# Adding the sums of the last down projection to the residual as each becomes whole, and moving the last norm's weights and factor one tile later

## The chip, the cores and the metric

The kernel runs on one core of a Trainium2 chip. The metric is device time in microseconds (us) of one execution. The engines are named as in the profile: PE is TensorE (matmuls; PEld its weight loads), DVE is VectorE, ACT is ScalarE, POOL is GpSimd, SP is SyncE, which here only issues DMAs. Each engine runs its instructions in order and waits on semaphores for the others. A change of 0.2% of the time, 1.7 us, is about the least that counts below as different.

## The reference

One encoder layer for two groups of 256 tokens (512 rows of 1024 numbers, float32), with shared weights, and a norm behind it:

```python
def rms_norm(x, g):
    y = x * lax.rsqrt(jnp.mean(x * x, axis=-1, keepdims=True) + EPS)
    return y * g

x = x + merged @ w_out                       # merged: three gated attention branches
h2 = rms_norm(x, norm2_g)
x = x + jnp.square(jax.nn.relu(h2 @ w_up)) @ w_down
return rms_norm(x, final_norm_g)
```

All that the change touches lies in the last three lines: the MLP, from 1024 to 4096 hidden units and back, the residual add, and the final norm.

## The kernel before

The attention part ends near 515 us of the span. The MLP behind it goes through the 4096 hidden units in NC = 8 chunks `c` of 512. Each matmul operand is split into two parts, a high and a low one (`hi`, `lo`; tiles `w` for weights, `f` and `h` for activations), and a product takes three matmuls (`mm3`), so the low part of a weight block, made by DVE, must be there for the second matmul of the first group.

Per chunk, eight half steps h = 0 to 7 compute the hidden units (`up`, matmuls `ps<-h,w`). Between them the down projection of the chunk before is done (`product`, matmuls `ps<-w,f`, 12 for each of seven products): Strassen's scheme in Winograd's form, with the token rows in two halves and the output columns in two halves, so that the output is four blocks "11", "12", "21", "22" (row half, column half), each of two row tiles of 128. The seven products go to four pairs of PSUM banks; a second product adds onto a bank pair that DVE has read before. `add_to` adds a bank to one of the sums in SBUF: "11", "12", "21" (tiles `acc`), "V" and "G", where V belongs to three outputs: 12 + V, 21 - V and 22 = G + V. The additions are put in the list `later` and are issued behind the next matmuls (`flush`).

The down projection of the last chunk, c = 7, is done without that scheme (`last_down`): for column half `hh` = 0 and then 1, and row tiles t = 0 to 3, twelve matmuls of 512 columns each; the last of them, hh = 1 and t = 3, is cut into two parts of 256 columns.

The residual rows lie in DRAM (`x1d`) until `fetch_x1` loads them into four `blk` tiles, `xt[t]` with the two column halves, and the final norm's weights into `gf`. The rows lack the factor of the norm ahead of the MLP, which is applied to the sums instead: `scaled` is one DVE instruction, a SCALAR_TENSOR_TENSOR, y = src * rr[t] + y. `combine` first adds V to (or takes it from) a sum, a TENSOR_TENSOR `acc<-acc,acc`, and then calls `scaled` on the result:

```python
    SUMMED = {5: "22", 6: "12", 7: "11"}
...
            if n != "11":
                V.tensor_tensor(acc[k, i], acc[k, i], acc["V", i], op=ALU.subtract if n == "21" else ALU.add)
            scaled(xt[t][:, int(n[1]) - 1], t, acc[k, i])
```

So in chunk 7 the sums 22, 12 and 11 are combined at half steps 5, 6 and 7, and 21 behind the first `last_down`.

The end is `finish` for each tile and half, and `final` for each tile. `finish`: DVE adds the bank (`blk<-ps,rr,blk`), ACT squares it with a running sum (`junk<-blk`, into `fs`), and DVE multiplies by the norm's weights (`blk<-blk,gf`), which must wait until ACT has read the tile. `final`: DVE sums `fs` (TENSOR_REDUCE) and scales it (TENSOR_SCALAR), POOL raises it to -1/2 (`fr`), ACT multiplies column half 0 by it and DVE half 1 (`blk<-blk,fr`), and ACT and SP each issue the store of one half.

Order: DVE, ACT and PE keep the order in which the program is written; SP's DMAs stand where their buffers are expected to come free.

Of the kernel before, what the change touches and what calls it, by code (L numbers as in the profile page):

```python
# [16 lines left out]
P = 128  # L17
# [60 lines left out]
def encoder_kernel(ctx: ExitStack, tc: tile.TileContext, a: dict, out: bass.AP):  # L78
# [68 lines left out]
    def unit(fn, *srcs):  # L147
        units.append((fn, srcs))
# [687 lines left out]
    ss = const("ss", [P, NT, 2])  # L836
    rr = const("rr", [P, NT])
    fs = const("fs", [P, NT, 3])
# [20 lines left out]
    def inv_ms():  # L859
        V.tensor_tensor(rr, ss[:, :, 0], ss[:, :, 1], op=ALU.add)  # L860
        V.tensor_scalar(rr, rr, 1.0 / D, EPS, op0=ALU.mult, op1=ALU.add)
        V.reciprocal(rr, rr)

# [104 lines left out]
    def product(w, c, name):  # L968
        _, bk, to, sign = PRODUCTS[name]
        x = forms.pop((c, name))  # L970
        new = name in ("P1", "Q5", "Q6", "P7")
        for i in range(2):
            if new:
                banks[bk, i] = bank()
            p = banks[bk, i]
            for j in range(2):
                t = slice(j * S + i * P, j * S + (i + 1) * P)
                k = slice(j * 512, (j + 1) * 512)
                mm3(p, x[:, 0, t], x[:, 1, t], w[0][:, k], w[1][:, k], new and j == 0, j == 1, not new)
        flush(9)  # L980
        ps_ = [banks[bk, i] for i in range(2)]
        later.append(lambda: [add_to(to, i, ps_[i], ALU.add if sign > 0 else ALU.subtract) for i in range(2)])

# [10 lines left out]

    def scaled(y, t, src):
        V.scalar_tensor_tensor(y, src, rr[:, t:t + 1], y, op0=ALU.mult, op1=ALU.add)


    def combine(n):
        k = "G" if n == "22" else n  # L1000
        for i in range(2):
            t = 2 * (n[0] == "2") + i
            if n != "11":
                V.tensor_tensor(acc[k, i], acc[k, i], acc["V", i], op=ALU.subtract if n == "21" else ALU.add)
            scaled(xt[t][:, int(n[1]) - 1], t, acc[k, i])

# [7 lines left out]
    def last_down(hh, ts, n0=0, n1=512, part=0):  # L1014
# [35 lines left out]
    for c in range(NC):  # L1050
        for h in range(8):
            ff, half = 4 * c + h // 2, h % 2
            unit(lambda *w, ff=ff, half=half: up(w[0] if w else None, ff, half), *([(a["w_up"][ff],)] if half == 0 else []))
            if c == 0:
                unit(lambda h=h: turn_x1(h % 4, h // 4))
            if h == 1:
                unit(lambda c=c: load_blocks(c) if c < NC - 1 else fetch_x1())
            if c == NC - 1 and h == 6:
                unit(lambda: ahead.__setitem__(0, 2))
            if c == NC - 1 and h in SUMMED:  # L1060
                unit(lambda n=SUMMED[h]: later.append(lambda: combine(n)))
            if c and h < 7:
# [11 lines left out]
    unit(lambda: later.append(lambda: combine("21")))  # L1074
    for t in (2, 3):
# [83 lines left out]
```

## Time and profile before

| | |
|---|---|
| time, median of 3 runs | 865.38 us (865.13 to 866.48) |
| the profiled execution's own time | 866.86 us |
| its span, first to last instruction | 865.1 us |
| PE busy | 845.0 us, 98% |
| DVE busy | 464.4 us, 54% |
| ACT busy | 397.8 us, 46% |
| POOL busy | 215.8 us, 25% |
| granted TensorE clock, mean | 0.989 of full |

The span is what instructions cover; the execution's own time is 1.8 us more. Busy shares are means over all stages. What a stage is worth is read from the stage itself: which engine waits there, and for whom. Times in the trace count from the start of the span.

### The profile page before, as it was taken

The numbers are of one execution on the slowest core, as the hardware profiler recorded it, in microseconds if no ns is written. First come the engines' busy times: TensorE is split into PE (matmuls) and PEld (weight loads), VectorE is DVE, ScalarE is ACT, GpSimd is POOL, SyncE is SP. The second block draws the span as 40 slices with busy tenths as digits, with TensorE's granted clock in tenths as the row PEclk, the third lists the DMA queues.
The fourth block names the chain that finished last, engine by engine and source line by source line (L and its number), as shares of the span: only waits on it lengthen the run. The fifth ranks groups of instructions, "written<-read, shape, count | busy, mean of one in ns | idle before, by whom it ended". The sixth has DMA issues, their size and how long they took to land.

```text
span 865.1 us, 10788 instructions
## 1 busy us (share of the span) xinstructions
PE 845.0 (98%) x4080; PEld 703.2 (81%) x4080; DVE 464.4 (54%) x741; ACT 397.8 (46%) x690; POOL 215.8 (25%) x161
## 2 busy tenths in 40 slices
PE   9999999999999999999999999999999999999993
PEld 8788998888888888888887888888888888888882
DVE  6585535465453312333436551556767676666884
ACT  6455555566554433223224346564544445454523
POOL 2314545656557452211222000000000010100001
PEclk9999999999999999999999999999999999999997
DMA  8343223224331238422322446475647465745212
GB/s 283 114 123 100 67 93 95 89 74 115 96 107 54 69 111 277 124 80 92 122 87 74 154 129 204 103 200 122 183 110 195 105 188 126 181 131 145 74 50 97
DMA packets 47468, 106.87 MB, mean 124 GB/s; under 512 B 19358, under 2 KB 19604, under 8 KB 47416
## 3 DMA queue, kind: packets, MB, share of 16 engines
q1 hardware_dynamic: 39992, 85.69, 30.5%
q0 software_dynamic: 4256, 14.73, 9.6%
q10 hardware_dynamic: 3168, 5.77, 1.9%
q8 instruction: 32, 0.52, 0.3%
q14 instruction: 20, 0.16, 0.1%
HBM read 101.93 MB, written 4.24 MB: 123 GB/s over the span
## 4 chain that ended last, share of the span: by engine, by line
PE 76%; DVE 12%; ACT 6%; issue 3%; DMA 2%; POOL 0%; SPq 0%; POOLq 0%; DVEq 0%; ACTq 0%
PE ps L72 69%; DVE w L72 3%; PE sc L72 3%; PE o L72 2%; ACT w L72 2%; PE tp L72 2%; DVE blk L72 2%; DVE acc L72 2%; DMA mr<-in_memT 1%; DVE f L72 1%; DMA raw<-in_w_mem 1%; ACT sp L72 1%; ACT junk L72 1%; DVE sp L72 1%; ACT f L72 1%
## 5 line engine op out<-in xcount | busy, mean ns | idle before, releaser
L72 PE MATMUL ps<-x,w 128*128 128x512 f32 x1080 | 252.4, 391 | 0.0
L72 PEld LDWEIGHTS ps<-x,w 128*128 128x128 f32 x1080 | 200.8, 188 | 41.4
L72 PE MATMUL ps<-h,w 128*128 128x512 f32 x768 | 184.5, 390 | 0.0
L72 PEld LDWEIGHTS ps<-h,w 128*128 128x128 f32 x768 | 143.6, 188 | 29.6
L72 PE MATMUL ps<-w,f 128*128 128x512 f32 (+1 forms) x696 | 164.4, 387 | 1.4 <-DVE acc L72 1.0
L72 DVE TENSOR_TENSOR w<-raw,w 128x1024 fp32r<-128x1024 f32 (+1 forms) x79 | 96.3, 1223 | 115.2 <-ACT w L72 114.8
L72 PEld LDWEIGHTS ps<-w,f 128*128 128x128 f32 x696 | 128.5, 188 | 30.5 <-issue 3.4
L72 ACT ACTIVATE w<-raw 128x1024 fp32r<-128x1024 f32 (+2 forms) x116 | 119.7, 1037 | 21.8 <-DMA raw<-in_w_mem 7.4
L161 POOL TENSOR_TENSOR w<-raw,w 128x1024 fp32r<-128x1024 f32 (+1 forms) x37 | 87.4, 2362 | 120.2 <-ACT w L72 95.0
L72 DVE TENSOR_TENSOR w<-blk,w 128x1024 fp32r<-128x1024 f32 x49 | 59.4, 1223 | 48.7 <-ACT w L72 48.7
L921 POOL DMA_DIRECT2D blk<-in_w_dn x21 | 18.2, 866 | 240.7 <-DVE w L72 240.7
L72 DVE TENSOR_TENSOR acc<-acc,ps 128x512 f32<-128x512 f32 x88 | 56.7, 681 | 2.7 <-PE ps L72 2.7
L72 ACT ACTIVATE w<-blk 128x1024 fp32r<-128x1024 f32 x49 | 50.8, 1049 | 15.9 <-DMA blk<-in_w_dn 15.9
L72 ACT ACTIVATE sp<-sp,st 128x256 f32<-128x256 f32 (+1 forms) x48 | 25.8, 539 | 57.7 <-DVE st L72 57.7
L72 ACT ACTIVATE f<-f 128x512 fp32r<-128x512 f32 x28 | 17.7, 633 | 74.3 <-DVE f L72 74.3
L72 ACT ACTIVATE g<-ps 128x512 f32<-128x512 f32 x16 | 9.6, 598 | 86.9 <-PE ps L72 86.9
L72 DVE TENSOR_TENSOR sum<-o,lo 64x256 f32<-64x256 f32 x24 | 10.0, 418 | 66.4 <-ACT lo L72 66.3
L72 PE MATMUL ps<-mg,w 128*128 128x512 f32 x192 | 44.3, 390 | 1.5 <-ACT mg L72 0.9
L72 PEld LDWEIGHTS ps<-mg,w 128*128 128x128 f32 x192 | 36.0, 188 | 9.6 <-ACT mg L72 1.3
L72 ACT ACTIVATE r<-ps 128x512 f32<-128x512 f32 x32 | 18.9, 591 | 52.4 <-PE ps L72 52.4
L72 PE MATMUL ps<-w,x 128*128 128x384 f32 (+1 forms) x192 | 39.9, 363 | 0.0
L469 POOL TENSOR_TENSOR sp<-sp,st 128x512 f32<-128x512 f32 (+1 forms) x32 | 36.7, 1148 | 6.4 <-DVE st L72 3.5
(147 smaller groups left out, 957.0 us busy)
## 6 DMA issues: line engine op xcount, KB each, us to landing
raw<-in_w_up SPq DMA_DIRECT2D x32, 512.0 KB, 4.5
blk<-in_w_dn SPq DMA_DIRECT2D x28, 512.0 KB, 7.3
blk<-in_w_dn POOLq DMA_DIRECT2D x28, 512.0 KB, 5.7
raw<-in_w_g SPq DMA_DIRECT2D x24, 512.0 KB, 3.3
raw<-in_w_b SPq DMA_DIRECT2D x12, 512.0 KB, 3.3
raw<-in_w_bam SPq DMA_DIRECT2D x8, 512.0 KB, 3.2
raw<-in_w_o SPq DMA_DIRECT2D x8, 512.0 KB, 3.2
raw<-in_w_mem SPq DMA_DIRECT2D x7, 512.0 KB, 3.8
```

The lines of the kernel that those rows point to most:

```text
L72: return self.tc.keep_in_program_order(method(*args, **kw))
L161: sub[0].tensor_tensor(lo[:, c], raw[:, c], f(hi[:, c]), op=ALU.subtract)
L469: G.tensor_tensor(s[:, :, :w], s[:, :, :w], st[:, 6:8].unsqueeze(2).to_broadcast([P, 2, w]), op=ALU.mult)
L921: G.dma_start(src, block(c, n[1:]), accum_op=ALU.add)
```

## The change

Three things change in the MLP's end.

1. In chunk 7 the sums go into the residual one by one. The sums of chunks 0 to 5 for 12, 11 and 21 are added to `xt` at half steps 1, 2 and 3; V at steps 4 (to 12) and 5 (from 21, with a factor -rr, for which `rr` gets a second column); G at step 6; V to 22 behind the first `last_down`. The last chunk's own products for 11, 12 and 21 are added from their banks to `xt` directly, by `scaled`, and no longer to `acc`. No `acc<-acc,acc` is left.
2. `fetch_x1` is called at the end of chunk 6 rather than in step 1 of chunk 7.
3. `finish` no longer multiplies by `gf`. Half 0 is multiplied by `gained`, one tile later; half 1 in `scale_out`, by one SCALAR_TENSOR_TENSOR with both the factor and `gf`. `final` is split into `factor` and `scale_out`, and `scale_out` of a tile stands behind the `finish` of the next one.

```diff
+        r, n = rr[:, :, 0], rr[:, :, 1]
...
+        V.tensor_scalar(n, r, -1.0, None, op0=ALU.mult)
...
+        if c == NC - 2 and to in ("11", "12", "21"):
+            later.append(lambda: sum_in(to, lambda i: ps_[i]))
+        else:
+            later.append(lambda: [add_to(to, i, ps_[i], ALU.add if sign > 0 else ALU.subtract) for i in range(2)])
...
+    def scaled(y, t, src, less=0):
+        V.scalar_tensor_tensor(y, src, rr[:, t, less:less + 1], y, op0=ALU.mult, op1=ALU.add)
+
+    def sum_in(n, src, less=0):
+
         for i in range(2):
             t = 2 * (n[0] == "2") + i
-            if n != "11":
-                V.tensor_tensor(acc[k, i], acc[k, i], acc["V", i], op=ALU.subtract if n == "21" else ALU.add)
-            scaled(xt[t][:, int(n[1]) - 1], t, acc[k, i])
+            scaled(xt[t][:, int(n[1]) - 1], t, src(i), less)
+
+    def combine(n, k, less=0):
+        sum_in(n, lambda i: acc[k, i], less)
...
-            if hh and n1 == 512:
-                later.append(lambda t=t: final(t, 2 + part))
+        t = ts[-1]
+        if hh and not part:
+            later.append(lambda: scale_out(t - 1) if t else None)
+        if hh and n1 == 512:
+            later.append(lambda: factor(t, 2 + part))
+        if hh == 0 or t == 0:
+            later.append(lambda: gained(t + hh * NT - 1))
...
-        V.tensor_tensor(y, y, gf[0][:, hh, n0:n1], op=ALU.mult)
...
+    def gained(t):
+        y = xt[t][:, 0]
+        V.tensor_tensor(y, y, gf[0][:, 0], op=ALU.mult)
...
+    def scale_out(t):
+        r = fr[:, t:t + 1]
         A.activation(xt[t][:, 0], xt[t][:, 0], AF.Copy, scale=r)
-        V.tensor_scalar(xt[t][:, 1], xt[t][:, 1], r, None, op0=ALU.mult)
+        V.scalar_tensor_tensor(xt[t][:, 1], xt[t][:, 1], r, gf[0][:, 1], op0=ALU.mult, op1=ALU.mult)
...
-    SUMMED = {5: "22", 6: "12", 7: "11"}
+
+    SUMMED = {1: ("12", "12"), 2: ("11", "11"), 3: ("21", "21"), 4: ("12", "V"), 5: ("21", "V", 1), 6: ("22", "G")}
...
-            if h == 1:
-                unit(lambda c=c: load_blocks(c) if c < NC - 1 else fetch_x1())
+            if h == 1 and c < NC - 1:
+                unit(lambda c=c: load_blocks(c))
+            if h == 7 and c == NC - 2:
+                unit(fetch_x1)
```

Where the instructions stand, on DVE in steps 3 to 5 of chunk 7. First the kernel before; `acc_4663` and `acc_4665` are V, `acc_4760` and `acc_4762` are G, `ps_6703` and `ps_6710` the bank pair that the last product, matmuls `ps_6703<-w_6717,f_6700`, goes on to use, `w_6718` that product's low weights.

```order
L72 TENSOR_TENSOR w_6696<-raw_6694,w_6695 128x1024
L72 TENSOR_TENSOR f_6700<-u_6427,f_6700 128x512
L72 TENSOR_TENSOR w_6718<-blk_6240,w_6717 128x1024
L72 TENSOR_TENSOR acc_4760<-acc_4760,ps_6703 128x512
L72 TENSOR_TENSOR acc_4762<-acc_4762,ps_6710 128x512
L72 TENSOR_TENSOR acc_4760<-acc_4760,acc_4663 128x512
L72 SCALAR_TENSOR_TENSOR blk_6557<-acc_4760,rr,blk_6557 128x512
L72 TENSOR_TENSOR acc_4762<-acc_4762,acc_4665 128x512
L72 SCALAR_TENSOR_TENSOR blk_6559<-acc_4762,rr,blk_6559 128x512
L72 TENSOR_TENSOR w_6759<-raw_6757,w_6758 128x1024
```

The same place with the change; `acc_4664` and `acc_4666` are V now, `acc_4761` and `acc_4763` are G, and `blk_6488` to `blk_6494` the rows of tiles 0 to 3.

```order
L72 TENSOR_TENSOR w_6703<-raw_6701,w_6702 128x1024
L72 TENSOR_TENSOR f_6707<-u_6428,f_6707 128x512
L72 SCALAR_TENSOR_TENSOR blk_6488<-acc_4664,rr,blk_6488 128x512
L72 SCALAR_TENSOR_TENSOR blk_6490<-acc_4666,rr,blk_6490 128x512
L72 TENSOR_TENSOR w_6727<-blk_6241,w_6726 128x1024
L72 TENSOR_TENSOR acc_4761<-acc_4761,ps_6710 128x512
L72 TENSOR_TENSOR acc_4763<-acc_4763,ps_6717 128x512
L72 SCALAR_TENSOR_TENSOR blk_6492<-acc_4664,rr,blk_6492 128x512
L72 SCALAR_TENSOR_TENSOR blk_6494<-acc_4666,rr,blk_6494 128x512
L72 TENSOR_TENSOR w_6766<-raw_6764,w_6765 128x1024
```

Two additions of V now stand ahead of the last product's weights and of the reading of its bank pair; behind that pair four instructions became two.

DVE's last rows, from the last whole tile (t = 2, half 1) on. Before; `blk_6557` is tile 2, `blk_6559` tile 3, the `ps` their banks.

```order
L72 SCALAR_TENSOR_TENSOR blk_6557<-ps_6955,rr,blk_6557 128x512
L72 TENSOR_TENSOR blk_6557<-blk_6557,gf_6561 128x512
L72 TENSOR_REDUCE fr<-fs 128x1
L72 TENSOR_SCALAR fr<-fr 128x1
L72 TENSOR_SCALAR blk_6557<-blk_6557,fr 128x512
L72 SCALAR_TENSOR_TENSOR blk_6559<-ps_6979,rr,blk_6559 128x256
L72 TENSOR_TENSOR blk_6559<-blk_6559,gf_6561 128x256
L72 SCALAR_TENSOR_TENSOR blk_6559<-ps_6996,rr,blk_6559 128x256
L72 TENSOR_TENSOR blk_6559<-blk_6559,gf_6561 128x256
L72 TENSOR_REDUCE fr<-fs 128x1
L72 TENSOR_SCALAR fr<-fr 128x1
L72 TENSOR_SCALAR blk_6559<-blk_6559,fr 128x512
```

With the change; `blk_6490` is tile 1, `blk_6492` tile 2, `blk_6494` tile 3.

```order
L72 SCALAR_TENSOR_TENSOR blk_6492<-ps_6950,rr,blk_6492 128x512
L72 SCALAR_TENSOR_TENSOR blk_6490<-blk_6490,fr,gf_6496 128x512
L72 TENSOR_REDUCE fr<-fs 128x1
L72 TENSOR_SCALAR fr<-fr 128x1
L72 SCALAR_TENSOR_TENSOR blk_6494<-ps_6973,rr,blk_6494 128x256
L72 SCALAR_TENSOR_TENSOR blk_6492<-blk_6492,fr,gf_6496 128x512
L72 SCALAR_TENSOR_TENSOR blk_6494<-ps_6993,rr,blk_6494 128x256
L72 TENSOR_REDUCE fr<-fs 128x1
L72 TENSOR_SCALAR fr<-fr 128x1
L72 SCALAR_TENSOR_TENSOR blk_6494<-blk_6494,fr,gf_6496 128x512
```

The multiplications by `gf` behind ACT's square are gone, and a tile's scaling stands behind the next bank's addition.

SP's queue in chunk 7, the one place where it differs; first before, then with the change. `raw` are weights on their way in, `gf` the norm's weights.

```order
L165 DMA raw_6506<-in_w_up 128x1024
L990 DMA blk_6559<-x1d 128x1024
L165 DMA raw_6607<-in_w_up 128x1024
L165 DMA raw_6694<-in_w_up 128x1024
L992 DMA gf_6561<-in_gf 128x1024
```

```order
L165 DMA raw_6517<-in_w_up 128x1024
L995 DMA blk_6494<-x1d 128x1024
L997 DMA gf_6496<-in_gf 128x1024
L165 DMA raw_6610<-in_w_up 128x1024
L165 DMA raw_6701<-in_w_up 128x1024
```

The loads of the residual rows stay where they were; `gf` moved ahead of two loads of weights.

## Rows read from the trace of the kernel before

**Rows 1.** The page: the span and its instructions.

```profile
span 865.1 us, 10788 instructions
```

**Rows 2.** Busy time by stretch: length, PE, PEld, DVE, ACT, POOL, clock, DMA.

```profile
850.20:865.10 14.90, 0.00 (x0) 0.00 (x0) 5.92 (x17) 4.63 (x11) 1.66 (x3) 0.58 0.37 141
```

**Rows 3.** PE's timeline from chunk 7's last product: start, length, instruction, count.

```profile
822.23 2.88 PE L72 MATMUL ps<-w,f 128*128 128x512 f32 x12
...
827.67 22.50 PE L72 MATMUL ps<-w,f 128*128 128x512 f32 x108
...
846.91 3.26 PE L72 MATMUL ps<-w,f 128*128 128x512 f32 x25
```

**Rows 4.** DVE's timeline, 797 to 836 us; in brackets the idle time before, and its releaser.

```profile
798.50 0.69 DVE L72 TENSOR_TENSOR f<-u,f 128x512 fp32r<-128x512 f32 x1 [1.13 <-ACT f L72]
800.90 1.23 DVE L72 TENSOR_TENSOR w<-blk,w 128x1024 fp32r<-128x1024 f32 x1 [1.71 <-ACT w L72]
...
806.72 1.23 DVE L72 TENSOR_TENSOR w<-blk,w 128x1024 fp32r<-128x1024 f32 x1 [0.26 <-ACT w L72]
...
813.21 1.23 DVE L72 TENSOR_TENSOR w<-blk,w 128x1024 fp32r<-128x1024 f32 x1 [0.26 <-ACT w L72]
...
818.42 1.28 DVE L72 TENSOR_TENSOR acc<-acc,ps 128x512 f32<-128x512 f32 x2
819.61 0.69 DVE L72 TENSOR_TENSOR acc<-acc,acc 128x512 f32<-128x512 f32 x1
...
822.39 1.22 DVE L72 TENSOR_TENSOR w<-raw,w 128x1024 fp32r<-128x1024 f32 x1
...
825.32 1.22 DVE L72 TENSOR_TENSOR w<-raw,w 128x1024 fp32r<-128x1024 f32 x1
...
831.76 0.68 DVE L72 TENSOR_TENSOR f<-u,f 128x512 fp32r<-128x512 f32 x1
...
834.63 0.74 DVE L72 SCALAR_TENSOR_TENSOR blk<-ps,rr,blk 128x512 f32<-128x512 f32 x1
```

**Rows 5.** Timeline of all engines, 853 us to the end.

```profile
853.13 0.74 DVE L72 SCALAR_TENSOR_TENSOR blk<-ps,rr,blk 128x512 f32<-128x512 f32 x1
...
854.66 0.69 DVE L72 TENSOR_TENSOR blk<-blk,gf 128x512 f32<-128x512 f32 x1 [0.79 <-ACT junk L72]
...
858.29 0.48 DVE L72 SCALAR_TENSOR_TENSOR blk<-ps,rr,blk 128x256 f32<-128x256 f32 x1
858.80 0.42 ACT L72 ACTIVATE junk<-blk 128x256 f32<-128x256 f32 x1 [0.89 <-DVE blk L72]
...
859.34 0.42 DVE L72 TENSOR_TENSOR blk<-blk,gf 128x256 f32<-128x256 f32 x1 [0.57 <-ACT junk L72]
859.69 0.15 DVE L72 TENSOR_REDUCE fr<-fs 128x1 f32<-128x3 f32 x1
...
860.69 0.72 ACT L72 ACTIVATE blk<-blk,fr 128x512 f32<-128x512 f32 x1 [1.37 <-POOL fr L1036]
...
861.44 0.34 ACTq L72 DMA_DIRECT2D out<-blk  x1
```

**Rows 6.** DVE's groups by shape, 790 to 865 us: count, busy us, mean ns, idle before.

```profile
L72 DVE TENSOR_TENSOR acc<-acc,ps 128x512 f32<-128x512 f32 x14 | 8.9, 680 | 0.0
...
L72 DVE SCALAR_TENSOR_TENSOR blk<-acc,rr,blk 128x512 f32<-128x512 f32 x8 | 5.9, 750 | 0.2
...
L72 DVE TENSOR_TENSOR blk<-blk,gf 128x512 f32<-128x512 f32 x7 | 4.9, 694 | 5.5 <-ACT junk L72 5.5
...
L72 DVE TENSOR_SCALAR blk<-blk,fr 128x512 f32<-128x512 f32 x4 | 1.9, 486 | 2.7 <-POOL fr L1036 2.7
```

**Rows 7.** SP's queue, 777 to 794 us: issues of x1d, weights and gf.

```profile
777.39 0.32 SPq L990 DMA_DIRECT2D blk<-x1d  x1
779.72 10.75 SPq L165 DMA_DIRECT2D raw<-in_w_up  x2
790.52 0.42 SPq L992 DMA_DIRECT2D gf<-in_gf  x1
```

More of the change, by code (lines that the diff above doesn't have):

```diff
@@ L836, in encoder_kernel @@
     ss = const("ss", [P, NT, 2])
-    rr = const("rr", [P, NT])
+    rr = const("rr", [P, NT, 2])
     fs = const("fs", [P, NT, 3])
@@ L859, in inv_ms @@
     def inv_ms():
-        V.tensor_tensor(rr, ss[:, :, 0], ss[:, :, 1], op=ALU.add)
-        V.tensor_scalar(rr, rr, 1.0 / D, EPS, op0=ALU.mult, op1=ALU.add)
-        V.reciprocal(rr, rr)
+        r, n = rr[:, :, 0], rr[:, :, 1]
+        V.tensor_tensor(r, ss[:, :, 0], ss[:, :, 1], op=ALU.add)
+        V.tensor_scalar(r, r, 1.0 / D, EPS, op0=ALU.mult, op1=ALU.add)
+        V.reciprocal(r, r)
+        V.tensor_scalar(n, r, -1.0, None, op0=ALU.mult)
     UP, blocks = {}, {}
@@ L981, in product @@
         ps_ = [banks[bk, i] for i in range(2)]
-        later.append(lambda: [add_to(to, i, ps_[i], ALU.add if sign > 0 else ALU.subtract) for i in range(2)])
+        if c == NC - 2 and to in ("11", "12", "21"):
+            later.append(lambda: sum_in(to, lambda i: ps_[i]))
+        else:
+            later.append(lambda: [add_to(to, i, ps_[i], ALU.add if sign > 0 else ALU.subtract) for i in range(2)])
     xt, gf, kept = {}, [], {}
@@ L993, in fetch_x1 @@
         gf.append(g)
[L995 to L1000, printed above, removed]
+    def scaled(y, t, src, less=0):
+        V.scalar_tensor_tensor(y, src, rr[:, t, less:less + 1], y, op0=ALU.mult, op1=ALU.add)
+    def sum_in(n, src, less=0):
         for i in range(2):
             t = 2 * (n[0] == "2") + i
-            if n != "11":
-                V.tensor_tensor(acc[k, i], acc[k, i], acc["V", i], op=ALU.subtract if n == "21" else ALU.add)
-            scaled(xt[t][:, int(n[1]) - 1], t, acc[k, i])
+            scaled(xt[t][:, int(n[1]) - 1], t, src(i), less)
+    def combine(n, k, less=0):
+        sum_in(n, lambda i: acc[k, i], less)
     def down(p, t, hh, ks, n0=0, n1=512):
@@ L1029, in finish, with factor @@
         A.activation(h2("junk")[:, n0:n1], y, AF.Square, accum_out=fs[:, t, at_:at_ + 1])
-        V.tensor_tensor(y, y, gf[0][:, hh, n0:n1], op=ALU.mult)
-    def final(t, n):
+    def gained(t):
+        y = xt[t][:, 0]
+        V.tensor_tensor(y, y, gf[0][:, 0], op=ALU.mult)
+    def factor(t, n):
         r = fr[:, t:t + 1]
@@ L1060, in encoder_kernel @@
             if c == NC - 1 and h in SUMMED:
-                unit(lambda n=SUMMED[h]: later.append(lambda: combine(n)))
+                unit(lambda n=SUMMED[h]: later.append(lambda: combine(*n)))
             if c and h < 7:
@@ L1073, in encoder_kernel @@
          *[(block(NC - 1, n),) for n in ("11", "21")])
-    unit(lambda: later.append(lambda: combine("21")))
+    unit(lambda: later.append(lambda: combine("22", "V")))
     for t in (2, 3):
@@ L1082, in encoder_kernel @@
         unit(lambda n=part: last_down(1, (3,), 256 * n, 256 * n + 256, n))
-    unit(lambda: flush(9))
+    unit(lambda: (flush(9), scale_out(NT - 1)))
     run()
```

## The prediction

> **What bounds the kernel now.** First the span [rows 1], then the busy time by stretch, then the timelines of PE and DVE side by side. PE is busy for 98% of the span, so in most of it nothing but PE matters. The exception is the end: from 850.20 to 865.10 us PE does nothing, and DVE (5.92 us), ACT and POOL share the stretch at low busy shares [rows 2]. PE's last matmul ends at 846.91 + 3.26 = 850.17 [rows 3]. DVE begins to read that matmul's bank only at 858.29 [rows 5]. So the last 15 us are two things: 8.1 us in which DVE, which works in order, is still busy with earlier banks, and 6.8 us from there to the end of the span, a chain that any version must go through (add the bank, square, sum, power, scale, store, end of program).
>
> Why DVE is late: it reads the first bank of the last projection at 834.63 [rows 4], and from there each tile and half costs it an addition, a wait for ACT's square (5.5 us over seven additions of 512 columns) and a multiplication by the norm's weights, and each tile a wait for POOL's power besides (2.7 us in four) [rows 6]. That is more than the 2.72 us that PE needs for twelve matmuls (822.23 to 827.67 is two such rows [rows 3]): DVE falls behind, and the last whole tile's bank, full at 846.91 + 0.39 = 847.3, is read at 853.13 [rows 3, 5].
>
> PE itself loses a little here too: from 827.67 to 846.91 there are 83 starts (the row of 108 less the row of 25) [rows 3]. At 2.72/12 = 0.227 us they make 18.81, not 19.24: 0.43 us are lost. The place is the low part of the last hidden units, which DVE makes at 831.76 to 832.44 [rows 4]; PE wants it for the third of its matmuls on k = 3, the 21st, at 827.67 + 20 x 0.227 = 832.21, and 0.3 of the loss is this.
>
> **What the change does to DVE in chunk 7.** Count the instructions of 512 columns for the sums: before, 6 additions from a bank to `acc`, 6 of V, 8 `scaled`; after, 6 `scaled` from a bank and 14 from `acc`. 20 and 20. So no work vanishes; 6 TENSOR_TENSORs of 0.69 and 6 of 0.68 become SCALAR_TENSOR_TENSORs of 0.75 [rows 4, 6], and eight of the twenty move ahead, to half steps 1 to 4. Two of 0.68 take 1.19 start to start (818.42 to 819.61 [rows 4]): the next starts 0.08 before the end. So I count a pair of 0.75 as 1.34.
>
> I follow DVE's lag against the trace of before [rows 4]. The pair of step 1 goes into the idle 1.13 ahead of 798.50; the 0.2 left over ends in the 1.71 ahead of 800.90. The first product onto a bank is added by `scaled`: +0.13. The pair of step 2 has 0.26 + 0.1 idle time ahead of 806.72: lag 1.1. The pair of step 3: ACT's hidden units behind it are as late as DVE, and of the pair only some 0.05 more remains: lag 1.15 at 813.21. The pair of step 4 has no idle time: lag 2.5. Then it goes back: at 819.61 four instructions (2.78) become two (1.34): lag 1.05 at 822.39, 1.2 at 825.32 with the next bank pair. Between 826.46 and 831.76, eight instructions (5.30) become four (2.68): DVE is 1.4 us ahead at 831.76, at 830.34.
>
> Is PE held by this lag? Low weights of the last product but one: wanted at 822.23 - 5.44 + 0.23 = 817.0, done 813.21 + 1.15 + 1.23 = 815.6. Bank pair of the last product, which DVE must have read: wanted at 822.23 [rows 3], first half read at 818.42 + 2.5 + 0.68 = 821.6, **0.6 us to spare**, the tightest place. Weights of the last projection, second block: wanted at 827.67 + 7 x 0.227 = 829.26, done 825.32 + 1.2 + 1.22 = 827.74. All in time, so the cost is nothing, covered by PE's stream; without that cover each us of lag is a us. And the low part at 831.76 comes 1.4 us earlier, so PE's 0.43 loss goes. PE would end at 849.74.
>
> **What it does to DVE at the end.** The two weight splits behind follow at 830.94; the second waits for its load, which is issued when the buffer is free, 1.2 us later than before, and ends near 833.2. The first bank is added at 833.2 instead of 834.63. Then two additions (1.34), the multiplication of tile 0, which waits for ACT's square (1.53 behind the addition, as 853.13 to 854.66 [rows 5]), two additions of V, the third tile, the multiplication of tile 1: 838.0. Tile 3's bank is full at 827.67 + 48 x 0.227 + 0.16 = 838.7. **From here DVE waits for PE**, and has per tile of 2.72 us: addition 0.67, scaling of the tile before 0.67, sum and scale 0.36, and one `gained` in front of it at most.
>
> Is the fused scaling, two tensors and a factor, 0.75? No row has it with `gf`. Bounds: 0.49, the one-tensor scaling that it replaces, and 0.75, the `scaled` of the same size [rows 6]. I take 0.75, since it reads two tensors too. On the path it counts little: the store of half 0 waits for ACT's 0.72 [rows 5], and half 1's is issued by SP, 0.26 later than before, at the same time as ACT's; between 0 and 0.3 us, and I take 0. The Trainium skill, VectorE: DVE Perf Modes, "The perf-mode tier table", speaks against this fusion: float32 instructions on one SBUF tensor have a mode of twice the rate, those on two tensors have not. The trace agrees, 0.49 beside 0.69 [rows 6]; by the rule the sum below is at most 0.3 us too low, by the rows' 0.72 of ACT it stands.
>
> The last tiles: tile 2's bank is full when PE starts on the 256-column parts, at 846.91 + 0.39 - 0.43 = 846.87; added at 846.9; sum at + 1.53 = 848.45; factor ready 1.00 behind that, as 859.69 to 860.69 [rows 5]: 849.45. The first part's addition starts at 848.8; the scaling of tile 2 waits for its factor, 849.45 to 850.13; the last part's addition, whose bank was full at 849.79, starts at 850.13, **0.34 us late instead of 8.1**. ACT has the scaling of tile 2 (0.72) and its store's issue (0.34) ahead of the last square, so that starts at 850.98, not 850.64. The sum follows the square by 0.54 (858.80 to 859.34), without the multiplication that stood between (0.35); factor at 850.98 + 0.54 + 1.00 = 852.52.
>
> **The sum**, against ACT's last scaling at 860.69 [rows 5]: DVE's lateness, 8.08 to 0.34: -7.74; PE's loss: -0.43; the multiplication ahead of the last sum: -0.35; ACT's scaling and store ahead of the last square: +0.34. Together -8.2: 852.5, and with the 4.4 us from there to the end a span of 856.9. The profiled execution took 866.86 with a span of 865.1, and the median of the runs shown is 865.38; I take 8.2 off that: **857.2 us**.
>
> What I cost at nothing besides: the extra factor -rr (one small DVE instruction in chunk 0, some 0.15 us by its kin, under PE's stream); `fetch_x1`, whose loads stand where they stood, the last at 777.39, while the first addition into a row is at 797.3 [rows 4, 7]; POOL's four powers, same count; POOL's last block load, which is issued behind the split at 800.90, ahead of any lag.
>
> **The rivals.**
> *The early additions hold PE.* Against 0.6 us to spare, the eight additions of steps 1 to 4 would have to be 0.1 us longer each to cost 0.2, or the pair of step 1 find its idle time gone (another 1.3, cost 0.7). For it: four SCALAR_TENSOR_TENSORs now stand where idle time was only 0.26. Time 857.4 to 859.0; what PE loses, the end loses whole.
> *A new wait at the end.* ACT's queue holds square, scaling and store issue of two tiles; if the store issue or a power is later than in the rows, tile 2's scaling holds DVE ahead of the last addition. Each 0.3 us is 0.3 us: up to 858.5.
> *The change does not do it.* If DVE's waits were not what makes the end late but some fixed cost behind PE, the span would not move: 865. Against it: POOL's and ACT's waits are named in the rows, and the last bank waits 8.1 us for DVE alone.
> *Slower: `gf` blocks SP's queue.* Its load now stands ahead of two loads of weights, and it waits for a buffer that PE must have read. If the buffer came free late, the weights behind it would be late: they were issued at 779.72, and are needed by PE after 808. The load and the two splits take some 7 us, so it costs PE from a release after about 801, us for us; slower than before from a release after 809. Against it: in the trace `gf` goes out at 790.52 right behind the weights, with a buffer one step later in the rotation, and the built program's wait is for the 3448th of 3952 matmuls, 504 from the last, some 110 us before PE's end.
>
> **How the numbers follow.** My forecast, 856.5 to 857.9 us, has 0.72; PE held by the additions or a new wait, to 859.0, has 0.20 together; no effect 0.03; `gf` 0.03, slower; the remaining 0.02 lies below 856.5 or between 859 and 863. The range 856.3 to 859.0 holds the first two. Within 0.2% (1.7 us) is about what a measurement here cannot tell from no change; only the case of no effect falls there. Faster 0.94, same 0.03, slower 0.03.
>
> **What would show it.** Right: PE without a gap at 832 and done near 849.8; DVE idle, released by PE, ahead of each `blk<-ps,rr,blk` from 838 on; the last of them within 0.5 us of PE's end; no DVE wait for ACT's square but ahead of sums. Wrong: a PE wait for DVE's `acc` near 822; `blk<-ps` still following each other without a wait for PE; SP's weight loads later than 779.7 and 790.1.

## The result, and the profile after

The changed kernel takes 858.0 us (median of 4 executions, 857.19 to 859.08) against 865.9 for the kernel before on the same chip: a ratio of 0.991, 95% interval [0.989, 0.993]. Run once more, 857.58 against 865.22, again 0.991 [0.9895, 0.9925]. Predicted were 857.2, 856.3 to 859.0. The profiled execution took 859.08, with a span 7.8 us shorter than before [rows 1]. The page's first line, and the waits from 795 to 858 us (total, times, longest):

```profile
span 857.3 us, 10785 instructions
```

```profile
DVE blk L72 <- PE ps L72: 3.1, 4, 1.4
...
DVE fr L72 <- ACT junk L72: 1.7, 2, 0.9
...
DVE blk L72 <- POOL fr L1049: 0.9, 2, 0.7
...
PE ps L72 <- DVE acc L72: 0.2, 1, 0.2
```

Read the first of the waits: in the last projection DVE now waits for PE, four times. No DVE `blk` waits for ACT's square any more; before, seven additions had cost 5.5 us in such waits, and POOL's power 2.7 [rows 6]. PE's only wait in this stretch, 0.2, is at 794.91, ahead of the first addition that moved (797.27); the kernel before has the same wait, 0.17 at 794.93. Of the six banks from 838 on DVE waits for PE ahead of four (3.1 us in all); the two parts of 256 columns were whole before DVE came to them. The tail in which PE does nothing is about 7.6 us instead of 14.9 [rows 2]; by stretch (length, PE, PEld, DVE, ACT, POOL, clock, DMA):

```profile
849.60:857.30 7.70, 0.10 (x1) 0.00 (x0) 2.03 (x5) 2.18 (x6) 0.55 (x1) 0.67 0.48 183
```

PE's timeline, which answers to [rows 3]. The 108 matmuls are one row of 22.07, not 22.50, and the gap at 832 is gone:

```profile
822.19 2.88 PE L72 MATMUL ps<-w,f 128*128 128x512 f32 x12
...
827.63 22.07 PE L72 MATMUL ps<-w,f 128*128 128x512 f32 x108
```

DVE's timeline, for [rows 4]. Compare the starts of the same instructions: 806.72 is now 807.88, 813.21 is 814.36, the bank pair of 818.42 is at 820.89, 822.39 is 823.41, 825.32 is 826.47, the low part of 831.76 is at 830.25, and the first bank, read at 834.63 before, is read at 833.24:

```profile
807.88 1.22 DVE L72 TENSOR_TENSOR w<-blk,w 128x1024 fp32r<-128x1024 f32 x1
...
814.36 1.22 DVE L72 TENSOR_TENSOR w<-blk,w 128x1024 fp32r<-128x1024 f32 x1
...
820.89 1.28 DVE L72 TENSOR_TENSOR acc<-acc,ps 128x512 f32<-128x512 f32 x2
...
823.41 1.22 DVE L72 TENSOR_TENSOR w<-raw,w 128x1024 fp32r<-128x1024 f32 x1
...
826.47 1.22 DVE L72 TENSOR_TENSOR w<-raw,w 128x1024 fp32r<-128x1024 f32 x1
...
830.25 0.69 DVE L72 TENSOR_TENSOR f<-u,f 128x512 fp32r<-128x512 f32 x1
...
833.24 1.40 DVE L72 SCALAR_TENSOR_TENSOR blk<-ps,rr,blk 128x512 f32<-128x512 f32 x2
...
838.71 0.75 DVE L72 SCALAR_TENSOR_TENSOR blk<-ps,rr,blk 128x512 f32<-128x512 f32 x1 [0.66 <-PE ps L72]
```

The last tiles in the timeline of all engines, for [rows 5]. The last bank is added at 850.09, 0.39 behind PE's end (827.63 + 22.07 = 849.70); the time in brackets at 849.42 is the wait for tile 2's power that holds it:

```profile
846.88 0.75 DVE L72 SCALAR_TENSOR_TENSOR blk<-ps,rr,blk 128x512 f32<-128x512 f32 x1 [0.84 <-PE ps L72]
...
849.42 0.75 DVE L72 SCALAR_TENSOR_TENSOR blk<-blk,fr,gf 128x512 f32<-128x512 f32 x1 [0.27 <-POOL fr L1049]
...
850.09 0.48 DVE L72 SCALAR_TENSOR_TENSOR blk<-ps,rr,blk 128x256 f32<-128x256 f32 x1
850.57 0.34 ACTq L72 DMA_DIRECT2D out<-blk  x1
850.96 0.42 ACT L72 ACTIVATE junk<-blk 128x256 f32<-128x256 f32 x1 [0.41 <-DVE blk L72]
...
851.50 0.15 DVE L72 TENSOR_REDUCE fr<-fs 128x1 f32<-128x3 f32 x1 [0.93 <-ACT junk L72]
...
852.51 0.72 ACT L72 ACTIVATE blk<-blk,fr 128x512 f32<-128x512 f32 x1 [1.04 <-POOL fr L1049]
852.51 0.75 DVE L72 SCALAR_TENSOR_TENSOR blk<-blk,fr,gf 128x512 f32<-128x512 f32 x1 [0.66 <-POOL fr L1049]
853.26 0.37 ACTq L72 DMA_DIRECT2D out<-blk  x1
```

DVE's groups by shape, 790 to 857 us, for [rows 6]:

```profile
L72 DVE SCALAR_TENSOR_TENSOR blk<-ps,rr,blk 128x512 f32<-128x512 f32 x13 | 9.4, 748 | 3.1 <-PE ps L72 3.1
...
L72 DVE SCALAR_TENSOR_TENSOR blk<-blk,fr,gf 128x512 f32<-128x512 f32 x4 | 3.0, 749 | 0.9 <-POOL fr L1049 0.9
```

SP's queue, for [rows 7]. The load of `gf` is issued ahead of the two loads of weights, without a wait in front of it:

```profile
777.11 0.32 SPq L995 DMA_DIRECT2D blk<-x1d  x1
777.48 0.42 SPq L997 DMA_DIRECT2D gf<-in_gf  x1
779.44 11.00 SPq L165 DMA_DIRECT2D raw<-in_w_up  x2
```

### The profile page after: what moved, and what is told of

It reads as the page before. It is cut to its first block, busy times and chain, and to the rows that moved or that the text cites. A ratio compares the mean times of both kernels' runs of the same rounds, so it can differ in the third digit from the quotient of the medians.

```text
span 857.3 us, 10785 instructions
## 1 busy us (share of the span) xinstructions
PE 844.4 (99%) x4080; PEld 703.8 (82%) x4080; DVE 462.8 (54%) x737; ACT 397.1 (46%) x690; POOL 216.0 (25%) x161
## 4 chain that ended last, share of the span: by engine, by line
PE 84%; DVE 8%; ACT 5%; issue 2%; DMA 1%; POOL 0%; POOLq 0%; SPq 0%; DVEq 0%; ACTq 0%
PE ps L72 77%; PE sc L72 3%; PE o L72 2%; DVE w L72 2%; PE tp L72 2%; ACT w L72 2%; DVE f L72 1%; ACT sp L72 1%; DVE sp L72 1%; DMA mr<-in_memT 1%; ACT f L72 1%; DVE sq L72 0%; ACT r L72 0%; DVE mg L72 0%; DVE acc L72 0%
## 5 line engine op out<-in xcount | busy, mean ns | idle before, releaser
L72 DVE TENSOR_TENSOR acc<-acc,ps 128x512 f32<-128x512 f32 x82 | 52.9, 682 | 2.9 <-PE ps L72 2.9
```

The costliest lines, as they stand in the source:

```text
L72: return self.tc.keep_in_program_order(method(*args, **kw))
```

## The experiments

The theory (A) is that of the prediction: DVE's waits in the last projection made the end late, the new norm order removes them, the early sums take DVE out of the way of the low part, and the path behind PE is what is left. The rivals were that either part alone does it all, that the early sums cost PE something, and that the place of the loads matters.

Executions of one program differ by up to 2.5 us ahead of chunk 7 (the reason stands in the last section). So each kernel is measured from the first matmul of the last projection (start of the row of 108 matmuls), and all times in this table are us from there, of one profiled execution each. The medians stand beside it; in the comparisons with the experiments the kernel before took 865.1 to 865.2. By their medians the change, its repetition and experiments 2 and 5 to 9 (856.4 to 858.7) are hardly told apart; what parts them is read from the stretch to the end of the span. How well that repeats, four profiles with the same end show: 29.67 in the change and in experiments 5, 6 and 10.

| kernel | median us (executions) | that matmul at | PE's end | last bank added, behind PE's end | last scaling | end of span |
|---|---|---|---|---|---|---|
| before | 865.9 (4) | 827.67 | 22.50 | 8.12 | 33.02 | 37.41 |
| the change | 858.0 (4) | 827.63 | 22.07 | 0.39 | 24.87 | 29.67 |
| 1 early sums only | 862.28 (8) | 825.65 | 22.07 | 5.75 | 30.22 | 34.62 |
| 2 new norm order only | 857.64 (4) | 825.51 | 22.59 | 0.39 | 25.39 | 30.19 |
| 3 scaling not postponed | 859.18 (6) | 825.55 | 22.07 | 2.41 | 26.55 | 31.35 |
| 4 `gf` not moved | 859.33 (1) | 825.60 | 22.07 | 3.10 | 27.56 | 31.96 |
| 5 loads where they were | 857.68 (1) | 826.20 | 22.07 | 0.39 | 24.87 | 29.67 |
| 6 four additions more on DVE | 858.66 (1) | 827.22 | 22.07 | 0.39 | 24.87 | 29.67 |
| 7 last half multiplied beside the power | 856.59 (1) | 825.13 | 22.07 | 0.38 | 25.25 | 29.69 |
| 8 tile 2 scaled behind the last addition | 856.88 (5) | 825.12 | 22.07 | 0.04 | 24.18 | 28.98 |
| 9 as 8, last stores in pieces | 856.42 (5) | 826.85 | 22.07 | 0.04 | 24.59 | 28.85 |
| 10 the change again | 857.58 (5) | 827.38 | 22.07 | 0.38 | 24.87 | 29.67 |

"Last scaling" is the start of ACT's last one. The expectations of 1, 2, 3 and 6 name spans that start from the changed kernel's execution, with that matmul at 827.63; the spans of these runs' own profiles (860.3, 855.7, 856.9, 856.9) began the last projection up to 2.1 us earlier. Put on 827.63, the stretches of 1 to 3 make 862.25, 857.82 and 858.98, inside the ranges that were expected if the theory holds; for experiment 6 see there.

**1. The early sums alone.** The sums and the place of the loads are as in the change, the norm at the end is as before.

```diff
-            later.append(lambda: scale_out(t - 1) if t else None)
...
-            later.append(lambda: factor(t, 2 + part))
...
-            later.append(lambda: gained(t + hh * NT - 1))
+            if hh and n1 == 512:
+                later.append(lambda t=t: final(t, 2 + part))
...
+        V.tensor_tensor(y, y, gf[0][:, hh, n0:n1], op=ALU.mult)
```

> The early sums alone (points 1 and 2 of the change), with the old finish and final. Theory A (DVE was late because of its waits behind each bank, for ACT's square and POOL's power): the gain stays small. DVE reads the first bank at 833.2 instead of 834.6, saves two instructions for V (1.3 us), PE's loss of 0.4 goes, and DVE then falls behind as before: the last scaling 2.8 us earlier than before, near 858, span 861.5 to 863, and DVE still waits nine times for ACT's square, 5 to 7 us in all. Rival B (DVE was late because the sums stood in its queue ahead of the first banks): most of the gain is here, span 858 to 859.

Measured: 862.28 us, ratio 0.9966 [0.9956, 0.9977]; the last stretch 34.62, so 2.8 of the 7.7 us. PE's 0.43 is gone. The first bank is added 1.35 earlier (5.62 behind the first matmul instead of 6.97), and the last sum behind it is two instructions, not four (1.44): 1.35 + 1.44 - 0.43 = 2.36 of lateness less, and 8.12 became 5.75. The waits for ACT and POOL stayed as they were:

```profile
DVE blk L72 <- ACT junk L72: 6.9, 9, 0.8
...
DVE blk L72 <- POOL fr L1041: 2.7, 4, 0.7
```

**2. The norm's order alone.** The sums are as before, the end is as in the change.

```diff
+            later.append(lambda: scale_out(t - 1) if t else None)
...
+            later.append(lambda: factor(t, 2 + part))
...
+            later.append(lambda: gained(t + hh * NT - 1))
...
-        V.tensor_tensor(y, y, gf[0][:, hh, n0:n1], op=ALU.mult)
```

> The new order of the last norm alone (point 3), with the old sums at half steps 5 to 7 and behind the first last_down. Theory A: DVE, which reads the first bank 1.4 us later, makes that good on the banks that follow, and the last bank is read within 1 us of PE's end; PE keeps its loss of 0.4 at 832. Last scaling near 853, span 857.3 to 858.5, so nine tenths of the gain. Rival B: DVE is still 4 us or more late at the last bank, span 862 or more.

Measured: 857.64, ratio 0.9907 [0.9893, 0.992]; 30.19, so 7.2 of 7.7 us. The last bank is added as soon behind PE as with the whole change, though the first one is added 1.4 later (7.01 against 5.61): with DVE faster than PE, a start 1.4 us later did not matter. By time alone (857.64) this run is not apart from the whole change; what is missing in the stretch is PE's loss, still there at the 21st matmul: 22.59 - 22.07 = 0.52. PE's timeline:

```profile
825.51 4.70 PE L72 MATMUL ps<-w,f 128*128 128x512 f32 x20
830.39 17.71 PE L72 MATMUL ps<-w,f 128*128 128x512 f32 x88 [0.18 <-DVE f L72]
```

**3. The scaling not postponed.** The change, with `scale_out` of a tile right behind its `factor`.

```diff
-        if hh and not part:
-            later.append(lambda: scale_out(t - 1) if t else None)
...
-            later.append(lambda: factor(t, 2 + part))
+            later.append(lambda: (factor(t, 2 + part), scale_out(t)))
```

> The change, but each tile's scaling stands right behind its factor instead of behind the next tile's addition; the fused multiplication and the early sums stay. If the postponement is needed: DVE waits some 0.7 us for POOL's power in each of four tiles and needs 0.67 + 0.86 + 0.36 + 0.66 + 0.67 = 3.2 us for a tile against PE's 2.72, so it falls behind 0.5 a tile, the last scaling comes near 854.2 instead of 852.5, span 858.8 to 859.5. Rival: the 0.2 to 1.4 us that DVE waits for PE ahead of each bank hold it all, span within 0.4 of 857.3.

Measured: 859.18, ratio 0.9928 [0.9913, 0.9942]; 31.35, so postponing is worth 1.68 us. The last bank is added 2.41 behind PE's end. DVE waits for POOL's power four times again:

```profile
DVE fr L72 <- ACT junk L72: 3.0, 4, 0.8
DVE blk L72 <- POOL fr L1047: 2.7, 4, 0.7
DVE blk L72 <- PE ps L72: 2.1, 2, 1.4
```

**4. The multiplication by `gf` not moved.** The change, but `finish` multiplies behind the square, and half 1 is scaled by a TENSOR_SCALAR.

```diff
-            later.append(lambda: gained(t + hh * NT - 1))
...
+        V.tensor_tensor(y, y, gf[0][:, hh, n0:n1], op=ALU.mult)
...
-        V.scalar_tensor_tensor(xt[t][:, 1], xt[t][:, 1], r, gf[0][:, 1], op0=ALU.mult, op1=ALU.mult)
+        V.tensor_scalar(xt[t][:, 1], xt[t][:, 1], r, None, op0=ALU.mult)
```

> The new sums and the scaling one tile later stay; undone is the place of the multiplication by the final norm's weights alone: it stands behind the square of its own tile and half again, and the scaling of half 1 has one tensor. Theory A (the wait of that multiplication for ACT's square is what makes DVE late): DVE waits for ACT's square seven to nine times, 5 us or more, the last bank is added 3 to 4 us behind PE's end instead of 0.39, and the stretch from the first matmul of the last down projection to the end of the span is 33.0 to 33.5 us (29.67 in the changed kernel, 31.35 with the scaling alone not postponed). Rival R (once the scaling is postponed, what is left of DVE's waits lies beside PE's matmuls): the last bank is added within 0.5 us of PE's end and the stretch is 30.0 us or less.

Measured: 31.96. The mechanism is A's: nine waits for the square, and the last bank added 3.10 late, within A's 3 to 4. The stretch is more than 1 us shorter than A said. 0.4 of that is the end, 4.40 behind the last scaling as in the kernel before, and not 4.80; for the rest, the lateness came out near the low end of what A said. So moving `gf` into the postponed scaling is worth 2.29 us.

```profile
DVE blk L72 <- ACT junk L72: 6.7, 9, 0.8
...
DVE blk L72 <- POOL fr L1048: 0.7, 1, 0.7
```

**5. The loads where they were.**

```diff
-            if h == 1 and c < NC - 1:
-                unit(lambda c=c: load_blocks(c))
-            if h == 7 and c == NC - 2:
-                unit(fetch_x1)
+            if h == 1:
+                unit(lambda c=c: load_blocks(c) if c < NC - 1 else fetch_x1())
```

> The change with one part undone: the loads of the residual rows and of the final norm's weights are issued in step 1 of chunk 7 again, behind the weights, as before the change. Theory A (the move of the loads brings and costs nothing, since their data stand long before they are wanted): 43.9 us from the 300th matmul before the end to the first matmul of the last down projection, 29.7 us from there to the end of the span, both within 0.1 of the changed kernel. Rival R (the loads arrive too late for the first sum at half step 1, or push other loads): PE or DVE waits for a DMA in chunk 7, and one of the two stretches is longer by 0.3 us or more.

Measured: 43.93 us from the 300th matmul before PE's end to the last projection, as with the change, and 29.67 behind that. The place of the loads is worth nothing either way (one profile).

**6. Four additions more on DVE in half step 4.** Their result is not read by anything.

```diff
+    def extra():
+        e = h2("extra")
+        for _ in range(4):
+            V.tensor_tensor(e, acc["V", 0], acc["V", 1], op=ALU.add)
...
+            if c == NC - 1 and h == 4:
+                unit(lambda: later.append(extra))
```

> The change with four more DVE additions of 128x512 (0.60 each, 2.4 together, into a tile that nothing reads) in half step 4, ahead of the last product's weights and of the reading of its bank pair. In the change that pair was read 0.6 us before PE wanted it. If that was the tightest place and PE's stream is what sets the end, PE waits 1.8 us there for DVE's acc and the span grows by as much, to 859.1, give or take 0.4; the last bank is still read within 0.6 of PE's end. Rival: DVE's idle time later takes it up, span within 0.4 of 857.3.

Measured: the four took 2.78 from the first's start to the next instruction, 0.695 each and not the 0.60 assumed (all four write one tile; that this is the cause, no run shows). PE stood 2.04 us for DVE's `acc` and began the last product at 821.67 instead of 816.75 + 2.72 = 819.47, where the hidden units ahead of it end: 2.20 late, so 2.78 - 2.20 = 0.58 was spare. The product itself took 0.11 longer (824.50 - 821.67 = 2.83), and the last projection began 2.32 later against the 300th matmul before PE's end (46.25 us behind it, not 43.93). Behind that nothing changed: 29.67. Expected were a wait of 1.8 and a span of 859.1, give or take 0.4; put on 827.63 the span is 827.63 + 2.32 + 29.67 = 859.62, a little above, as the four took 0.38 longer than assumed. The span of this profile itself, 856.9, lies where the rival had it, but not for the rival's reason: DVE's idle time later took up none of the 2.32, and the granted clock from 40 to 60 us was 1.00 in this execution, 0.83 in the changed kernel's (see the last section).

```profile
821.67 2.98 PE L72 MATMUL ps<-w,f 128*128 128x512 f32 x12 [2.04 <-DVE acc L72]
```

**7. The last half multiplied beside the last power.** This parts the scaling of the last half 1 into a multiplication by `gf`, while POOL computes, and a scaling with one tensor.

```diff
+        if t == NT - 1:
+            V.tensor_tensor(xt[t][:, 1], xt[t][:, 1], gf[0][:, 1], op=ALU.mult)
...
+        if t < NT - 1:
+            V.scalar_tensor_tensor(xt[t][:, 1], xt[t][:, 1], r, gf[0][:, 1], op0=ALU.mult, op1=ALU.mult)
+        else:
+            V.tensor_scalar(xt[t][:, 1], xt[t][:, 1], r, None, op0=ALU.mult)
```

> The change, but for the last tile the multiplication of column half 1 by the norm's weights stands right behind the sum and scale, beside POOL's last power, and the scaling behind it has one tensor (0.49 us, not 0.75), so that SP issues its store 0.26 us ahead of ACT's rival store. Theory L (a DVE instruction with two tensors in SBUF holds POOL's power: 0.94 instead of 0.55 us): the last power is 0.9 us or more, ACT's last scaling comes 0.3 to 0.4 us later against the first matmul of the last down projection, and the stretch from there to the end of the span is 29.6 to 29.9 us (29.67 in the changed kernel). Rival N (the long power of tile 0 has another cause, such as its place in POOL's program): the last power stays at 0.55 to 0.6, ACT's last scaling stands where it stood, and the stretch is 29.3 to 29.5 us, as the two last stores no longer start together.

Measured: theory L. The power took 0.93 and the last scaling came 0.38 later; the stores, issued 0.24 apart, gave 0.36 back (4.44 behind the last scaling, not 4.80): 29.69. All engines, the last lines:

```profile
849.26 0.68 DVE L72 TENSOR_TENSOR blk<-blk,gf 128x512 f32<-128x512 f32 x1
849.42 0.93 POOL L1049 TENSOR_TENSOR fr<-fr,mhalf 128x1 f32<-128x1 f32 x1 [2.53 <-DVE fr L72]
850.38 0.72 ACT L72 ACTIVATE blk<-blk,fr 128x512 f32<-128x512 f32 x1 [1.42 <-POOL fr L1049]
850.38 0.49 DVE L72 TENSOR_SCALAR blk<-blk,fr 128x512 f32<-128x512 f32 x1 [0.44 <-POOL fr L1049]
850.89 0.33 SPq L1061 DMA_DIRECT2D out<-blk  x1
851.13 0.34 ACTq L72 DMA_DIRECT2D out<-blk  x1
```

**8. Tile 2 scaled behind the last addition**, and both its stores issued by SP.

```diff
-        if hh and not part:
-            later.append(lambda: scale_out(t - 1) if t else None)
+        if hh and (part if t == NT - 1 else t):
+            later.append(lambda: scale_out(t - 1))
...
-            (A, SP)[hh].dma_start(out[t * P:(t + 1) * P, hh * 512:(hh + 1) * 512], xt[t][:, hh])
+            (SP if t == NT - 2 else A, SP)[hh].dma_start(out[t * P:(t + 1) * P, hh * 512:(hh + 1) * 512], xt[t][:, hh])
```

> The change with its last tiles in another order: the scaling of tile 2 and its two stores stand behind the addition of the last part's bank, not ahead of it, and SP issues both of these stores, so that ACT's last square has neither that scaling nor a store's issue ahead of it. Theory A (in the changed kernel the last addition waits 0.34 us for tile 2's scaling, and the last square 0.34 for a store's issue): the last bank is added 0.1 us or less behind PE's end, ACT's last scaling comes 0.6 us earlier against the first matmul of the last down projection, 24.3 instead of 24.87, and the stretch to the end of the span is 29.0 to 29.2 us: a time 0.5 to 0.7 us below the changed kernel's. Rival R (tile 2's scaling now stands in ACT's or DVE's way behind the last square): the sum or the last scaling waits for it, and the stretch is 29.5 us or more.

Measured: 28.98, 0.69 less than the change; 856.88 us, ratio 0.9905 [0.989, 0.992], which by time alone can't be told from the change's 0.991. The last addition follows PE's end by 0.04, and the last square follows that addition by 0.52 instead of 0.87. All engines:

```profile
847.23 0.48 DVE L72 SCALAR_TENSOR_TENSOR blk<-ps,rr,blk 128x256 f32<-128x256 f32 x1 [0.59 <-PE ps L72]
847.63 0.74 DVE L72 SCALAR_TENSOR_TENSOR blk<-blk,fr,gf 128x512 f32<-128x512 f32 x1
847.75 0.42 ACT L72 ACTIVATE junk<-blk 128x256 f32<-128x256 f32 x1 [0.34 <-DVE blk L72]
```

**9. The last stores in pieces.** As 8, and the last tile's halves are scaled and stored in pieces of 256 columns, three stores by SP and the last of half 0 by ACT.

```diff
+        for n in range(2):
+            c = slice(256 * n, 256 * n + 256)
+            A.activation(xt[t][:, 0, c], xt[t][:, 0, c], AF.Copy, scale=r)
+            V.scalar_tensor_tensor(xt[t][:, 1, c], xt[t][:, 1, c], r, gf[0][:, 1, c], op0=ALU.mult, op1=ALU.mult)
+            for hh in range(2):
+                (A if n else SP, SP)[hh].dma_start(out[t * P:(t + 1) * P, hh * 512 + 256 * n:hh * 512 + 256 * n + 256], xt[t][:, hh, c])
```

> The reordered tail of the previous runs (tile 2's scaling and stores behind the last addition), and the last tile's two column halves are scaled and stored in two pieces of 256 columns each, so that its first store is issued about 0.27 us earlier (a scaling of 256 columns takes 0.48, one of 512 takes 0.75). Theory B (the two last stores move 0.5 MB through the same DMA engines at about 0.38 MB per us, so the last byte lands 2.7 to 2.8 us behind the first of their issues, whichever comes first): the stretch from the first matmul of the last down projection to the end of the span is 28.7 to 28.8 us, against 28.98 with whole halves. Rival S (each store has a latency of its own behind its own issue, and more issues and smaller packets add to it): the last of the four is issued no earlier than before, and the stretch is 29.0 us or more.

Measured: 28.85, between the two: 0.13 gained, not 0.25. The first store goes out 0.54 behind the start of the scaling (851.02 to 851.56) instead of 0.75, but SP's three issues stand at 851.56, 851.99 and 852.49, and the piece for the third had been ready since 851.90. The last byte lands 3.10 behind the first issue, so theory B does not hold for four stores. It lands no earlier than in 8 at all: 27.81 us from the first matmul of the last projection, against 27.76. The 0.13 lies behind the landing, 1.04 to the end of the span instead of 1.22, and why, no run here tells. SP's issues and GB/s, 848.0 to 855.7 in 40 slices:

```profile
851.56 1.33 SPq L1064 DMA_DIRECT2D out<-blk  x3
```

```profile
GB/s 0 21 372 351 372 319 351 426 383 128 0 0 0 0 0 223 362 383 426 362 362 372 266 309 293 282 346 330 346 335 346 107 0 0 0 0 0 0 0 0
```

While the pieces move, 852.4 to 854.0, the rate is 282 to 346 GB/s; with whole halves it was some 380 (the change's DMA view in the next section). At the mean of these slices, 323, the 0.52 MB of the four takes some 0.25 us longer than at 380 (an estimate from these rates), about the 0.27 by which 3.10 is more than the 2.83 of two whole stores. How much of that is the smaller packets and how much SP's queue, these rows do not part. The median is 856.42 us, ratio 0.9897 [0.988, 0.9914]: the lowest of all, though not apart from 8 by time.

**10. The changed kernel again.**

> The changed kernel itself, once more. Theory C (two executions of one program differ by up to 2.5 us ahead of chunk 7 by how long TensorE's granted clock stands at its low level between 39 and 47 us, and by nothing behind it): from the first matmul of the last down projection to the end of the span 29.67 us again, within 0.1, wherever that matmul stands between 824.9 and 827.7; at 827.6 if the clock between 40 and 60 us is 0.83 on average, at about 825 if it is 1.00. Rival D (the end varies from execution to execution by as much as the times do): the stretch differs from 29.67 by 0.3 us or more.

The kernel is the changed one as it stands. Measured: 29.67 to the hundredth, with the first matmul of the last projection at 827.38 and a clock of 0.83 between 40 and 60 us: theory C.

## Why the prediction was right

The times below are compared as they stand, without a correction, because the two profiled executions begin the last projection at nearly the same time, 827.67 and 827.63. That is luck: other executions begin it up to 2.5 us earlier.

- **DVE's lag in chunk 7.** Said 1.1, 1.15, 2.5, 1.05, 1.2 late and then 1.4 early; measured 1.16, 1.15, 2.47, 1.02, 1.15 late and 1.51 early. The counting of instructions, 1.34 for a pair of 0.75 and 1.19 for a pair of 0.68, held everywhere.
- **0.6 us to spare at the last product.** The first of the bank pair was read by 820.89 + 0.68 = 821.57, and PE began at 822.19: 0.62. Experiment 6 confirms it from outside: 2.78 us put in front made PE 2.20 late.
- **PE's 0.43 goes.** 22.50 became 22.07; experiment 2, without the early sums, keeps the loss. PE's end said 849.74, measured 849.70.
- **From tile 3 on DVE waits for PE.** Said from 838.7; the first such wait ends at 838.71. The sign "ahead of each bank" held for four banks of six; the last two came as the prediction's own times had them, without a wait for PE.
- **The fused scaling at 0.75.** Measured 0.749, at the upper bound. The 0.49 of the scaling with one tensor [rows 6] is lost. That loss counts more than the prediction took it to, see the mis-sized term.
- **The last tiles.** Addition of tile 2 said 846.9, measured 846.88; its factor 849.45, 849.42; the last addition 850.13, 850.09; the last square 850.98, 850.96; the last scaling 852.52, 852.51. The last addition is 0.39 behind PE's end, as 850.13 was behind the 849.74 forecast. Experiment 8 takes away both waits that were costed here, twice 0.34, and gains 0.69.
- **The mis-sized term: the end of the stores**, "between 0 and 0.3 us, and I take 0". It measured 0.4: the span ends 4.80 behind the last scaling, before 4.40. ACT and SP now issue the last two stores at 853.26 and 853.29, and these land at 856.09 and 855.91; before, SP's was issued at 861.20 and ACT's at 861.44, and they landed at 863.21 and 863.92. The prediction took ACT's store as the one that counts, which goes out 0.75 behind the scaling in both. What counts is the first issue: 861.20 to 863.92 is 2.72, 853.26 to 856.09 is 2.83. Before, that was SP's, 0.51 behind the scaling; now SP waits for the longer fused scaling, and ACT's is the first, 0.75 behind. So 0.24 of the 0.40 is the first issue, 0.11 the two stores that meet, and 0.05 lies behind the landing (1.16 and 1.21 to the end). The DMA view, 850.0 to 857.3 in 40 slices (busy share of the 16 DMA engines in tenths, and GB/s), shows both stores moving through them at once, nine tenths busy, at some 380 GB/s, from 854.2 to 855.5:

```profile
DMA  9993029999999200000000299999992000000000
GB/s 404 359 382 101 0 101 370 438 382 359 382 370 393 79 0 0 0 0 0 0 0 0 112 426 382 393 370 370 393 359 68 0 0 0 0 0 0 0 0 0
```

  Experiment 7 brings the two issues apart again and 0.36 back. Of the 0.8 us by which the median missed, these 0.4 are one half; the other is the median of before, 865.9 in this comparison and 865.38 in the one that the prediction started from. In the repetition, 857.58 against 865.22, the miss is the 0.4 alone.
- **The rivals.** The early additions did not hold PE: from the 300th matmul before PE's end to the last projection it is 43.93 us with the change and 43.95 before. The wait at the end that the sum had costed is there, and no longer than said. `gf` did not block SP's queue: it was issued at 777.48 without a wait, and experiment 5 shows that its place is worth nothing.
- **Where the range was lucky.** The median, 858.0, lies 0.1 above the inner forecast of 856.5 to 857.9, in the part that was held for a rival, though no rival came true. And the four executions run from 857.19 to 859.08, the profiled one outside the range: a spread from the start of the program (up to 2.5 us, last section) that the prediction did not reckon with, and that is about as wide as the range of 2.7.
- **The shares.** Against the whole change, leaving out the postponed scaling costs 1.68, the moved `gf` 2.29, the early sums 0.52; the first two, left out together, cost 4.95 (experiment 1), more than their sum of 3.97. So parts that relieve one in-order engine don't add here; the likely reason, which no run tests by itself, is that what is left of the lateness counts only where DVE is still slower than PE.

## What to carry to other kernels

Work that an in-order engine does behind the last matmul is best read as a rate: what it needs per tile, with its waits, against what PE needs. Once it is below, as here, the end is PE's end and a fixed chain; a start 1.4 us earlier bought DVE nothing more (experiment 2). Put the instruction that waits for another engine one tile later, behind work that is ready, and then look at what stands ahead of the very last addition and the very last square, a postponed scaling and a store's issue here (0.69 us). When two engines share a last store, start one early: with issues 0.03 to 0.24 us apart the pair was done 2.7 to 2.8 us behind the first issue (two times 256 KB). Smaller stores did not land earlier: four of 128 KB took 3.10.

## What was not expected of the hardware

**POOL's power takes longer beside one kind of DVE instruction.** In the changed kernel the power of tile 0 takes 0.94 us and the others 0.55 or 0.56. It starts while DVE multiplies two tensors in SBUF (843.23 to 843.91); the one at 848.84 runs beside an addition from a PSUM bank (848.68) and isn't slowed. POOL's timeline:

```profile
843.40 0.94 POOL L1049 TENSOR_TENSOR fr<-fr,mhalf 128x1 f32<-128x1 f32 x1 [40.06 <-DVE fr L72]
...
848.84 0.55 POOL L1049 TENSOR_TENSOR fr<-fr,mhalf 128x1 f32<-128x1 f32 x1 [2.16 <-DVE fr L72]
```

Experiment 7 put such a multiplication beside the last power and made it 0.93; in experiments 1, 3 and 4, which have none beside tile 0's power, that one took 0.57. The Trainium skill, SBUF — State Buffer, "Who interferes with whom", says that a DVE instruction with two SBUF inputs contends with a GpSimd instruction that reads SBUF, because its second input comes through the read interface that the two engines share. The traces agree in kind: 0.94 against 0.55. In the changed kernel it costs nothing, as tile 0's factor is not waited for.

**Most of the spread between executions lies in 8 us near the start.** In the changed kernel's profile the granted clock is 0.50 (1.2 of 2.4 GHz) from 40 to 46 us; in that of experiment 8, whose program is the same there, it is 1.00 there, and its last projection begins at 825.12, not 827.63. PE's pair of one-column matmuls ahead of that stretch begins 0.18 apart in the two executions (39.01 and 38.83), the second row of `w,m` behind it 2.56 apart (47.64 and 45.08), and the last projection 2.51 apart. What PE does ahead of it is the same in both, 16 matmuls of one column at 39 us. Busy time by stretch, first the changed kernel, then experiment 8 (the clock is the first number behind POOL's):

```profile
42.00:44.00 2.00, 2.00 (x7) 1.71 (x7) 0.22 (x2) 0.00 (x0) 1.98 (x4) 0.50 0.55 211
44.00:46.00 2.00, 2.00 (x6) 1.52 (x6) 1.77 (x2) 0.00 (x0) 2.00 (x5) 0.50 0.05 12
```

```profile
42.00:44.00 2.00, 1.98 (x9) 1.29 (x7) 0.23 (x1) 0.00 (x0) 1.98 (x4) 1.00 0.59 234
44.00:46.00 2.00, 1.49 (x5) 0.93 (x6) 1.59 (x2) 0.32 (x1) 2.00 (x5) 1.00 0.07 15
```

Over the eleven profiles other than experiment 6 (which adds to chunk 7), the two with a clock of 1.00 between 40 and 60 us begin the last projection at 825.1, the four at 0.83 to 0.85 at 826.9 to 827.7, and the five at 0.91 in between. Why the clock falls in one execution and not in the next, no run here tells.
